# GLA layer of a two-block transformer: modulation of the first 128 features on TensorE, load order, and order of the projections

## Chip, cores and metric

The kernel runs on one core of one Trainium2 chip. The metric is the device time of one execution in microseconds (us); lower is better. A change of 0.2% is about what three runs can tell from none.

## The reference, cut to what matters

Five layers run one after the other over a sequence of 512 rows of 1024 features: gated linear attention (GLA), a gated MLP with a short convolution, a retention layer, a shared key/value projection with latent attention, and their norms. Only the first, GLA, is touched. What it computes, shortened:

```
cs = silu(c)                                          # 1024 numbers
shift, scale, gate = split(cs @ mod_w[0,0] + mod_b[0,0], 3)
h = x * (1 + scale) + shift                           # (512, 1024)
q, k, v, r, a_lr = split(h @ w_in, [512, 1024, 2048, 3072])
log_a = log_sigmoid(a_lr @ w_a2 + b_a) / 16           # the gates, 4 heads x 128
q_dec = q * 128**-0.5 * exp(cumsum(log_a)); k_inv = k * exp(-cumsum(log_a))
o = causal(q_dec k_inv^T) v + q_dec S                 # S: state carried from chunk to chunk, per head
u = o * rsqrt(mean(o*o) + 1e-5) * norm_g * silu(r)    # heads of 256 columns
y = layer_norm(2**0.25 * x + (1 + gate) * (u @ w_o))
```

All products keep FP32 accuracy: each operand is split into a high and a low part in the FP32R format, and three matmuls (high x high, high x low, low x high) make one product.

## The kernel before

Engines run side by side, each through its own instruction stream in a fixed order; a scheduler places the instructions when the kernel is built, by priority in program order and by its own estimates, so an instruction that the program writes later may run in a gap of an earlier part. The order in which the Python code issues the parts is therefore the lever that the change pulls.

**Matrix products.** `mm3` (L152) issues the three matmuls, at L154, L155 and L156. `wload` (L120) loads 512 KB of weights into a `raw` tile on the SP queue (L127), and `split` (L107) makes the high part by a cast on ScalarE (L114) and the low part by a subtraction on VectorE (L115) into a `wsp` tile. There are four `raw` and four `wsp` buffers (L266), and each is reused in program order: a load waits until the tile four places back has been consumed. `proj_t` (L169) multiplies four blocks of 128 rows by 512 weight columns into four accumulators `acc`; `proj_f` (L201) makes tiles of 128 features by 512 rows. After the first stage there are four `acc` and four `aux` PSUM banks. A projection of 512 columns is 96 matmuls of 512 columns.

**The first stage** is `gla_start` (L484): eight slices k of 128 features. For each, `loads` (L494) issues the slice of the modulation weights `ms` (two halves of 512 KB, L498), of the transposed input `xq` (256 KB, L499) and of `l_w` (512 KB, L501), which holds the weight columns of v (heads 0 and 1), and of q and k (heads 0 and 1). `operand` (L504) computes scale and shift of the 128 features on VectorE, as a sum over `ms` times the row `csr` = silu(c), broadcast to all partitions (L508), adds the bias `mb` into `mc` (L510, L511) and lets ScalarE make the high part of the operand, `hT`, and the full value `xv` (L516); L517 makes the low part. `weights` casts and splits `raw`. Then come 24 matmuls into eight accumulators. `setup` (L296) loads `csr` first of all and applies silu to it (L301); `setup_late` (L310) loads and transforms `cs`, the same numbers as columns, after the stage.

**The rest of GLA** is issued by `gla` (L382) in this order: `gla_a` (the 16 gate columns), `gla_decay` (L581: the gate chain, that is exp, ln, scan and exp on ScalarE and VectorE for four heads), `gla_r` of pair 0 with its Silu on ScalarE (L418), `vectors` (L317), `gla_prep` of heads 0 and 1, `gla_inner` of head 0 (L640), `gla_qk` of head 2, `gla_inner` of head 1, `gla_qk` of head 3, `gla_outer` of heads 0 and 1 (L672), `gla_prep` of 2 and 3, `gla_v` of pair 1, `gate_T` of pair 0 (transposes, L442, and splits, L117 and L118), `gla_inner` of 2 and 3, `gla_r` of pair 1 (L462), the reload of x (L466), `gla_outer` of 2 and 3, `gate_T` of pair 1, and the output projection in `post_mod` (L692). `gla_inner` has a serial part: the state `sf` goes from chunk to chunk (L665, L666) and is split into `st`.

Between these, `place` (L402) hands out ten pieces of modulation work: eight chunks for the next layer, each two loads of 512 KB into `raw` and two VectorE sums (L411), and two gate chunks of 512 columns (`mod_chunk`, L349), each four loads and eight VectorE steps (L362). `PLACE` (L269) says how many go where.

Of the kernel before, what the change touches and what calls it, by code (L numbers as in the profile page):

```python
# [18 lines left out]
P = 128  # L19
T = 512  # L20
# [47 lines left out]
def layouts(ins):  # L68
# [4 lines left out]
    def mod(i):  # L73
# [5 lines left out]
    m0, m1 = mod(0), mod(1)  # L79
    return {"l_ba": np.ascontiguousarray(ins["gla_b_a"][0].reshape(4, P).T),  # L80
            "l_x": np.ascontiguousarray(ins["x"][0].T),
            "l_mod": m0[0], "l_modb": m0[1], "l_mod1": m1[0], "l_modb1": m1[1],
# [14 lines left out]
class Kern:  # L97
# [168 lines left out]
    RAW, WSP, ST, MS = 4, 4, 6, 4  # L266
    GATES = {0: 4, 1: 5, 2: 6, 3: 7}
    WOUT = {6: (0, 2), 7: (2, 4)}
    PLACE = (0, 2, 0, 2, 2, 2, 2)  # L269
# [26 lines left out]
    def setup(self, ph):  # L296
        nc, a = self.nc, self.a
        cr = a["c"][0]
        self.csr = self.mod.tile([P, D], F32, name="csr")
        nc.sync.dma_start(self.csr, bass.AP(tensor=cr.tensor, offset=cr.offset, ap=[[0, P], [1, D]]))  # L300
        nc.scalar.activation(self.csr, self.csr, AF.Silu)  # L301
# [7 lines left out]

    def setup_late(self, ph):  # L310

        nc, a = self.nc, self.a
        self.cs = self.cons.tile([P, 8], F32, name="cs")
        nc.sync.dma_start(self.cs, a["l_c"])
        nc.scalar.activation(self.cs, self.cs, AF.Silu)
# [66 lines left out]
    def gla(self):  # L382
        nc, a, tc = self.nc, self.a, self.tc
        w = a["gla_w_in"][0]
        with ExitStack() as ctx:
# [38 lines left out]
            with tc.tile_pool(name="gla_core", bufs=1, reuse_waits="tile") as ph:  # L424
# [6 lines left out]
                def prep(h):  # L431
                    return self.gla_prep(ph, decay[h], raw[h])
# [13 lines left out]
                p0 = prep(0)  # L446
                p1 = prep(1)
                place(3)
                i0 = self.gla_inner(ph, p0, vh(0), tril)
                raw += self.gla_qk(xT, (2,))  # L450
                i1 = self.gla_inner(ph, p1, vh(1), tril)
                raw += self.gla_qk(xT, (3,))
# [9 lines left out]
                self.gla_r(xT, 1, lambda b, ps: nc.scalar.activation(u[1][:, b, :], ps, AF.Silu))  # L462
                place(6)
                for b in range(NB):
                    self.res[b] = self.main.tile([P, D], F32, tag=f"res{b}", name=f"res{b}")
                    nc.sync.dma_start(self.res[b], a["x"][0, b * P:(b + 1) * P, :])  # L466
                outer(2, i2)
# [13 lines left out]
            self.post_mod(lambda n: (uP, self.wsubs(a["gla_w_o"][0], n * 512, n * 512 + 512,  # L481
                                                    pool=self.tail if n else None)), 8, gate, True, A, B)

    def gla_start(self, ph, out):  # L484
# [4 lines left out]
        accs = [self.acc() for _ in range(8)]  # L489
        mb = ph.tile([P, 8, 2], F32, name="mb")  # L490
        nc.sync.dma_start(mb, a["l_modb"].rearrange("p (k j) -> p k j", j=2))
# [818 lines left out]
```

## Time and profile before

| what | us |
|---|---|
| median of 3 runs | 1260.5 |
| lowest and highest run | 1259.19 and 1261.57 |
| the profiled execution, its own time | 1261.78 |
| its span, from the first to the last instruction | 1260.0 |
| TensorE (PE) busy | 1225.5 (97% of the span) |
| VectorE (DVE) busy | 817.6 (65%) |
| ScalarE (ACT) busy | 535.3 (42%) |
| DMA | 118 GB/s mean over the span |

The profile is of one execution; 1.8 us of its time lie outside the span. PE counts matmuls, PEld the loading of their stationary operand, SPq the issue of DMAs on the SyncE queue. PEclk is the granted TensorE clock as a part of 2.4 GHz (0.5 is 1.2 GHz). In a timeline a line is: start, duration, engine, source line, operation, output<-inputs, count, and in brackets the idle time before it with what ended it. A line marked x4 merges four instructions that follow each other.

### The profile page before, as it was taken

To read this page: it belongs to the slowest core of one execution; us is meant where nothing else is said; L and a number is where in the kernel's file an instruction comes from. 1 tells how busy PE (TensorE), PEld (TensorE's weight loads), DVE (VectorE), ACT (ScalarE), POOL (GpSimd) and SP (SyncE) were. 2 spreads that over 40 slices of the span, in tenths; PEclk is the share of its full clock that TensorE was granted. 3 is DMA by queue.
4 is the path that set the end of the run, shared out by engine and by line. 5 is a ranking of instruction groups with operands and counts; after the bars stand their busy time and mean duration, and the time that the engine had idled before them with its cause. 6 is when DMAs were issued, how large, how long until landed. Compare 5 with 4: busy or idle time off the path is not lost.

```text
span 1260.0 us, 16047 instructions
## 1 busy us (share of the span) xinstructions
PE 1225.5 (97%) x5982; PEld 1024.9 (81%) x5982; DVE 817.6 (65%) x1836; ACT 535.3 (42%) x946; POOL 3.7 (0%) x15
## 2 busy tenths in 40 slices
PE   5989999999999999999999999999999999999997
PEld 4767877898888888888788888888888888888886
DVE  5698877788442354445875649556454689687755
ACT  3583444533332223341543333433434347577631
POOL 0000000000000000000000000000000000000000
PEclk9998999999999999999999999999999999999999
DMA  9658554147322333333152332323332333212221
GB/s 346 213 171 258 168 195 134 51 125 226 97 90 98 101 99 89 97 134 117 66 158 86 88 90 82 92 85 92 117 106 96 109 98 107 69 50 78 84 84 68
DMA packets 133043, 148.44 MB, mean 118 GB/s; under 512 B 9825, under 2 KB 92152, under 8 KB 132964
## 3 DMA queue, kind: packets, MB, share of 16 engines
q1 hardware_dynamic: 132964, 147.40, 36.5%
q8 instruction: 47, 0.77, 0.3%
q14 instruction: 32, 0.26, 0.1%
HBM read 141.09 MB, written 6.29 MB: 117 GB/s over the span
## 4 chain that ended last, share of the span: by engine, by line
PE 86%; DVE 7%; ACT 4%; DMA 2%; issue 2%; SPq 0%; DVEq 0%; ACTq 0%
PE acc L154 25%; PE acc L156 25%; PE acc L155 25%; PE po L154 1%; PE po L156 1%; PE po L155 1%; PE aux L154 1%; PE aux L156 1%; PE aux L155 1%; DMA raw<-in_gla_w_in 1%; DVE wsp L115 1%; PE aux L899 1%; DMA ms<-in_l_mod 1%; ACT wsp L114 1%; PE aux L1251 1%
## 5 line engine op out<-in xcount | busy, mean ns | idle before, releaser
L115 DVE TENSOR_TENSOR wsp<-raw,wsp 128x1024 fp32r<-128x1024 f32 (+1 forms) x162 | 195.5, 1208 | 192.4 <-ACT wsp L114 192.1
L114 ACT CAST wsp<-raw 128x1024 fp32r<-128x1024 f32 (+1 forms) x162 | 167.9, 1039 | 289.5 <-PE acc L156 253.6
L154 PE MATMUL acc<-hT,wsp 128*128 128x512 f32 (+1 forms) x640 | 244.8, 382 | 0.5 <-DVE v L115 0.5
L156 PE MATMUL acc<-hT,wsp 128*128 128x512 f32 (+1 forms) x640 | 243.7, 381 | 0.0
L155 PE MATMUL acc<-hT,wsp 128*128 128x512 f32 (+1 forms) x640 | 243.3, 380 | 0.0
L154 PE MATMUL acc<-wsp,hT 128*128 128x512 f32 (+2 forms) x448 | 170.0, 386 | 14.6 <-ACT wsp L114 14.6
L155 PE MATMUL acc<-wsp,hT 128*128 128x512 f32 (+2 forms) x448 | 171.6, 383 | 0.0
L156 PE MATMUL acc<-wsp,hT 128*128 128x512 f32 (+2 forms) x448 | 170.3, 382 | 0.0
L154 PEld LDWEIGHTS acc<-hT,wsp 128*128 128x128 f32 x640 | 121.2, 189 | 23.7 <-DVE v L115 1.4
L155 PEld LDWEIGHTS acc<-hT,wsp 128*128 128x128 f32 x640 | 120.9, 189 | 22.1 <-issue 0.2
L156 PEld LDWEIGHTS acc<-hT,wsp 128*128 128x128 f32 x640 | 120.8, 189 | 22.0
L154 PEld LDWEIGHTS acc<-wsp,hT 128*128 128x128 f32 x448 | 84.7, 189 | 29.9 <-ACT wsp L114 14.6
L156 PEld LDWEIGHTS acc<-wsp,hT 128*128 128x128 f32 x448 | 84.6, 189 | 15.1
L155 PEld LDWEIGHTS acc<-wsp,hT 128*128 128x128 f32 x448 | 84.7, 189 | 14.4 <-DVE wsp L115 0.3
L154 PE MATMUL acc<-wsp,uT 128*128 128x512 f32 (+1 forms) x192 | 75.3, 392 | 0.0
L156 PE MATMUL acc<-wsp,uT 128*128 128x512 f32 (+1 forms) x192 | 75.2, 392 | 0.0
L155 PE MATMUL acc<-wsp,uT 128*128 128x512 f32 (+1 forms) x192 | 74.9, 390 | 0.0
L154 PE MATMUL acc<-wsp,p 128*128 128x512 f32 x144 | 56.9, 395 | 0.0
L155 PE MATMUL acc<-wsp,p 128*128 128x512 f32 x144 | 56.9, 395 | 0.0
L156 PE MATMUL acc<-wsp,p 128*128 128x512 f32 x144 | 56.9, 395 | 0.0
L801 DVE SCALAR_TENSOR_TENSOR cv<-acc,cols,cv 128x511 f32<-128x511 f32 x22 | 16.5, 749 | 57.7 <-ACT cv L800 57.7
L800 ACT ACTIVATE cv<-acc,cols 128x512 f32<-128x512 f32 x22 | 17.2, 780 | 82.4 <-PE acc L156 82.4
(357 smaller groups left out, 2062.1 us busy)
## 6 DMA issues: line engine op xcount, KB each, us to landing
raw<-in_w_in_a SPq DMA_DIRECT2D x48, 512.0 KB
raw<-in_ffn_w_up SPq DMA_DIRECT2D x44, 512.0 KB
raw<-in_ffn_w_down SPq DMA_DIRECT2D x22, 512.0 KB
ms<-in_l_mod SPq DMA_DIRECT2D x16, 512.0 KB
raw<-in_gla_w_in SPq DMA_DIRECT2D x16, 512.0 KB
rawm<-in_l_mod SPq DMA_DIRECT2D x16, 512.0 KB
rawm<-in_mod_w SPq DMA_DIRECT2D x16, 512.0 KB
raw<-in_w_out_a SPq DMA_DIRECT2D x16, 512.0 KB
```

Source lines behind the costliest of these rows:

```text
L114: nc.scalar.copy(hi, src)
L115: nc.vector.tensor_sub(lo, src, self.f(hi))
L154: mm(out, l[0], r[0], start=first, stop=False)
L155: mm(out, l[0], r[1], start=False, stop=False)
L156: mm(out, l[1], r[0], start=False, stop=last)
L800: nc.scalar.activation(t, p, AF.Identity, scale=cw[2 * NT + j], bias=cb[j])
L801: nc.vector.scalar_tensor_tensor(t[:, 1:], p[:, :T - 1], cw[NT + j], t[:, 1:], op0=OP.mult, op1=OP.add)
L899: nc.tensor.transpose(pu[:, b * P:(b + 1) * P], u[:, b, i * P:(i + 1) * P], self.ident)
L1251: nc.tensor.matmul(sc[:, :n], qrT[i][:, s], kr[i][:, :n], start=False, stop=i == 1)
```

## The change

Six edits, all in GLA. (1) The scale and shift of the first 128 features are computed on TensorE: a new array `l_f0` holds the modulation weights of these features as eight blocks of 128 inputs for scale and eight for shift, and 16 plain F32 matmuls of one column multiply them with `cs`. `setup_late` goes; `cs` and the bias `mb` are loaded on ScalarE's queue at the start. (2) The SP queue of the start takes `l_f0` (two halves), the first slice of x, the first weight slice in two halves, and only then `csr`; the first slice's casts are done in halves and its matmuls ordered by the part that is ready. (3) Twelve matmuls of 512 columns on a constant tile run ahead of the first loads' arrival (`WARM`). (4) `gla_qk` of heads 2 and 3 moves in front of `gla_prep` of 0 and 1; `gla_r` of pair 1 moves from behind `gla_inner` of 3 to behind `gla_inner` of 1. (5) The first half of the output projection's first 512 columns (features from pair 0) is issued between `gla_inner` of 3 and `gla_outer` of 2, into accumulators that `post_mod` then goes on with. (6) `PLACE` changes from (0, 2, 0, 2, 2, 2, 2) to (2, 0, 0, 0, 3, 3, 2).

```diff
--- before.py
+++ after.py
@@ -77,8 +77,10 @@
         return np.ascontiguousarray(both), np.ascontiguousarray(bias.transpose(1, 0, 2).reshape(P, 16))
 
     m0, m1 = mod(0), mod(1)
+    f0 = np.concatenate([ins["mod_w"][0, 0][:, 1024:1024 + P], ins["mod_w"][0, 0][:, 0:P]], 1)
     return {"l_ba": np.ascontiguousarray(ins["gla_b_a"][0].reshape(4, P).T),
             "l_x": np.ascontiguousarray(ins["x"][0].T),
+            "l_f0": np.ascontiguousarray(f0.reshape(8, P, 2 * P).transpose(1, 0, 2).reshape(P, 16 * P)),
             "l_mod": m0[0], "l_modb": m0[1], "l_mod1": m1[0], "l_modb1": m1[1],
             "l_c": np.ascontiguousarray(ins["c"].reshape(8, P).T),
             "l_w": np.ascontiguousarray(np.concatenate([w[:, 1024:1536], w[:, 0:256], w[:, 512:768]], 1))}
@@ -264,9 +266,10 @@
 
 
     RAW, WSP, ST, MS = 4, 4, 6, 4
+    WARM = 12
     GATES = {0: 4, 1: 5, 2: 6, 3: 7}
     WOUT = {6: (0, 2), 7: (2, 4)}
-    PLACE = (0, 2, 0, 2, 2, 2, 2)
+    PLACE = (2, 0, 0, 0, 3, 3, 2)
 
     def run(self):
         tc, nc = self.tc, self.nc
@@ -295,10 +298,10 @@
 
     def setup(self, ph):
         nc, a = self.nc, self.a
-        cr = a["c"][0]
         self.csr = self.mod.tile([P, D], F32, name="csr")
-        nc.sync.dma_start(self.csr, bass.AP(tensor=cr.tensor, offset=cr.offset, ap=[[0, P], [1, D]]))
-        nc.scalar.activation(self.csr, self.csr, AF.Silu)
+        self.cs = self.cons.tile([P, 8], F32, name="cs")
+        nc.scalar.dma_start(self.cs, a["l_c"])
+        nc.scalar.activation(self.cs, self.cs, AF.Silu)
         self.ident = self.cons.tile([P, P], F32, name="ident")
         make_identity(nc, self.ident)
         self.rstd = self.cons.tile([P, NB], F32, name="rstd")
@@ -306,13 +309,6 @@
         nc.gpsimd.memset(self.ones, 1.0)
         self.res = [None] * NB
         self.col = {}
-
-    def setup_late(self, ph):
-
-        nc, a = self.nc, self.a
-        self.cs = self.cons.tile([P, 8], F32, name="cs")
-        nc.sync.dma_start(self.cs, a["l_c"])
-        nc.scalar.activation(self.cs, self.cs, AF.Silu)
 
     def vectors(self, ph):
 
@@ -443,13 +439,12 @@
                         self.split(t[:, 0, i, :], t[:, 1, i, :], pu, scale=self.c("norm_g")[i % 2])
                     return t
 
-                p0 = prep(0)
-                p1 = prep(1)
+                raw += self.gla_qk(xT, (2, 3))
                 place(3)
+                p0, p1 = prep(0), prep(1)
                 i0 = self.gla_inner(ph, p0, vh(0), tril)
-                raw += self.gla_qk(xT, (2,))
                 i1 = self.gla_inner(ph, p1, vh(1), tril)
-                raw += self.gla_qk(xT, (3,))
+                self.gla_r(xT, 1, lambda b, ps: nc.scalar.activation(u[1][:, b, :], ps, AF.Silu))
                 place(4)
                 outer(0, i0)
                 outer(1, i1)
@@ -459,11 +454,13 @@
                 uT = [gate_T(0)]
                 i2 = self.gla_inner(ph, p2, vh(2), tril)
                 i3 = self.gla_inner(ph, p3, vh(3), tril)
-                self.gla_r(xT, 1, lambda b, ps: nc.scalar.activation(u[1][:, b, :], ps, AF.Silu))
                 place(6)
                 for b in range(NB):
                     self.res[b] = self.main.tile([P, D], F32, tag=f"res{b}", name=f"res{b}")
                     nc.sync.dma_start(self.res[b], a["x"][0, b * P:(b + 1) * P, :])
+
+                accs = [self.acc() for _ in range(NB)]
+                self.proj_t(self.pair_of(uT), self.wsubs(a["gla_w_o"][0], 0, 512, 0, 4), 512, None, accs=accs)
                 outer(2, i2)
                 outer(3, i3)
                 uT.append(gate_T(1))
@@ -478,8 +475,9 @@
             nc.vector.tensor_mul(B, self.col["ln_b0"], mc1[:, :, 0])
             nc.vector.tensor_add(B, B, mc1[:, :, 1])
             gate = self.mod_gate([mods[0, 2048], mods[0, 2560]])
-            self.post_mod(lambda n: (uP, self.wsubs(a["gla_w_o"][0], n * 512, n * 512 + 512,
-                                                    pool=self.tail if n else None)), 8, gate, True, A, B)
+            wo = a["gla_w_o"][0]
+            first = ((k + 4, w) for k, w in self.wsubs(wo, 0, 512, 4, 8))
+            self.post_mod(lambda n: (uP, self.wsubs(wo, 512, 1024, pool=self.tail) if n else first), 8, gate, True, A, B, accs=accs)
 
     def gla_start(self, ph, out):
 
@@ -487,13 +485,54 @@
         nc, a = self.nc, self.a
         tl, xT = self.new_hT()
         accs = [self.acc() for _ in range(8)]
+
+        warm = ph.tile([P, T], F32R, tag="t2", name="warm", bufs=2)
+        nc.vector.tensor_copy(warm, self.ones[:, 0:1].to_broadcast([P, T]))
+        for _ in range(self.WARM):
+            nc.tensor.matmul(accs[7], warm[:, :P], warm, start=True, stop=True)
         mb = ph.tile([P, 8, 2], F32, name="mb")
-        nc.sync.dma_start(mb, a["l_modb"].rearrange("p (k j) -> p k j", j=2))
         xs = [self.main.tile([P, 2, T], F32, tag=f"res{q}", name=f"xq{q}") for q in range(4)]
+
+        def first():
+
+            m = ph.tile([P, 8, 2, P], F32, tag="ms", name="m0", bufs=self.MS)
+            f0 = a["l_f0"].rearrange("p (k j f) -> p k j f", k=8, j=2)
+            raw = self.main.tile([P, self.WN], F32, tag="raw", name="raw", bufs=self.RAW)
+            for k in (0, 4):
+                nc.sync.dma_start(m[:, k:k + 4], f0[:, k:k + 4])
+            nc.scalar.dma_start(mb, a["l_modb"].rearrange("p (k j) -> p k j", j=2))
+            nc.sync.dma_start(xs[0][:, 0], a["l_x"][0:P])
+            halves = [slice(0, 512), slice(512, D)]
+            for h in halves:
+                nc.sync.dma_start(raw[:, h], a["l_w"][0:P, h])
+            cr = a["c"][0]
+            nc.sync.dma_start(self.csr, bass.AP(tensor=cr.tensor, offset=cr.offset, ap=[[0, P], [1, D]]))
+            pm = [accs[6 - j][:, 0:1] for j in range(2)]
+            for k in range(8):
+                for j in range(2):
+                    nc.tensor.matmul(pm[j], m[:, k, j], self.cs[:, k:k + 1], start=k == 0, stop=k == 7)
+            mc = self.small(2, "mc")
+            nc.vector.tensor_scalar(mc[:, 0:1], pm[0], mb[:, 0, 0:1], 1.0, op0=OP.add, op1=OP.add)
+            nc.vector.tensor_add(mc[:, 1:2], pm[1], mb[:, 0, 1:2])
+            hi, lo = tl[0][:, 0, 0, :], tl[0][:, 1, 0, :]
+            sp = self.main.tile([P, 2, self.WN], F32R, tag="wsp", name="wsp", bufs=self.WSP)
+            v = ph.tile([P, T], F32, tag="t2", name="xv", bufs=2)
+            nc.scalar.activation(hi, xs[0][:, 0], AF.Identity, scale=mc[:, 0:1], bias=mc[:, 1:2])
+            for h in halves:
+                nc.scalar.copy(sp[:, 0, h], raw[:, h])
+                nc.vector.tensor_sub(sp[:, 1, h], raw[:, h], self.f(sp[:, 0, h]))
+            nc.scalar.activation(v, xs[0][:, 0], AF.Identity, scale=mc[:, 0:1], bias=mc[:, 1:2])
+            nc.vector.tensor_sub(lo, v, self.f(hi))
+            parts = [([t[:, b * P:(b + 1) * P] for t in xT.k[0]], [sp[:, i, 0:512] for i in range(2)]) for b in range(NB)]
+            parts += [([sp[:, i, 512 + j * P:640 + j * P] for i in range(2)], xT.k[0]) for j in range(4)]
+            order = [[(0, 0), (0, 1), (1, 0)]] * NB + [[(0, 0), (1, 0), (0, 1)]] * 4
+            for t in range(3):
+                for acc, (l, r), o in zip(accs, parts, order):
+                    nc.tensor.matmul(acc, l[o[t][0]], r[o[t][1]], start=t == 0, stop=False)
 
         def loads(k):
             r = slice(k * P, k * P + P)
-            m = ph.tile([P, 2, D], F32, tag="ms", name="ms", bufs=4)
+            m = ph.tile([P, 2, D], F32, tag="ms", name="ms", bufs=self.MS)
             for j in range(2):
                 nc.sync.dma_start(m[:, j], a["l_mod"][r, j * D:(j + 1) * D])
             nc.sync.dma_start(xs[k // 2][:, k % 2], a["l_x"][r])
@@ -521,15 +560,17 @@
             self.split(sp[:, 0], sp[:, 1], raw)
             return sp
 
-        for k in range(8):
+        first()
+        nc.scalar.activation(self.csr, self.csr, AF.Silu)
+        for k in range(1, 8):
             m, raw = loads(k)
             operand(k, m)
             sp = weights(raw)
             wv = [sp[:, i, 0:512] for i in range(2)]
             for b in range(NB):
-                self.mm3(accs[b], [t[:, b * P:(b + 1) * P] for t in xT.k[k]], wv, k == 0, k == 7)
+                self.mm3(accs[b], [t[:, b * P:(b + 1) * P] for t in xT.k[k]], wv, False, k == 7)
             for j in range(4):
-                self.mm3(accs[4 + j], [sp[:, i, 512 + j * P:640 + j * P] for i in range(2)], xT.k[k], k == 0, k == 7)
+                self.mm3(accs[4 + j], [sp[:, i, 512 + j * P:640 + j * P] for i in range(2)], xT.k[k], False, k == 7)
         v = out.tile([P, 2, NB, 512], F32R, tag="v", name="v")
         for b in range(NB):
             self.split(v[:, 0, b, :], v[:, 1, b, :], accs[b])
@@ -539,7 +580,6 @@
             for j in range(2):
                 nc.scalar.copy(raw[:, j], accs[4 + 2 * j + h])
             raws.append(raw)
-        self.setup_late(ph)
         return xT, v, raws
 
     def gla_v(self, out, xT, pr):
@@ -689,7 +729,7 @@
         for b in range(NB):
             nc.vector.scalar_tensor_tensor(u[:, b], out[b], rs[:, b:b + 1], u[:, b], op0=OP.mult, op1=OP.mult)
 
-    def post_mod(self, src, nk, gate, alpha, A, B=None, affine=None):
+    def post_mod(self, src, nk, gate, alpha, A, B=None, affine=None, accs=None):
 
 
 
@@ -741,7 +781,7 @@
                 self.res_rstd(b)
 
         xP, subs = src(0)
-        self.proj_t(xP, subs, 512, lambda b, p: z_half(b, 0, p), nk=nk)
+        self.proj_t(xP, subs, 512, lambda b, p: z_half(b, 0, p), nk=nk, accs=accs)
         xP, subs = src(1)
         self.proj_t(xP, subs, 512, lambda b, p: (z_half(b, 1, p), finish(b)), nk=nk, tail=4)
 
```

## Rows read from the trace of the kernel before

**Rows 1.** The page, busy time (us), share of the span and instructions of TensorE.

```profile
PE 1225.5 (97%) x5982; PEld 1024.9 (81%) x5982; DVE 817.6 (65%) x1836; ACT 535.3 (42%) x946; POOL 3.7 (0%) x15
```

**Rows 2.** Waits of TensorE, whole span: waiter, releaser, total us, times, longest.

```profile
PE acc L154 <- ACT wsp L114: 14.6, 1, 14.6
PE aux L154 <- ACT ki L114: 4.2, 1, 4.2
PE aux L154 <- ACT kt L114: 2.6, 1, 2.6
...
PE aux L154 <- DVE sf L665: 0.7, 1, 0.7
```

**Rows 3.** Stretches of 2 us: busy us of PE, PEld, DVE, ACT, POOL, PEclk, DMA.

```profile
90.00:92.00 2.00, 0.01 (x1) 0.01 (x1) 2.00 (x5) 2.00 (x5) 0.00 (x0) 0.71 0.55 137
...
96.00:98.00 2.00, 2.00 (x11) 1.90 (x11) 1.33 (x4) 1.29 (x2) 0.00 (x0) 0.59 1.07 363
...
114.00:116.00 2.00, 1.65 (x8) 1.56 (x9) 2.00 (x4) 1.33 (x3) 0.00 (x0) 0.68 0.82 269
116.00:118.00 2.00, 2.00 (x8) 1.71 (x8) 1.33 (x3) 0.41 (x1) 0.00 (x0) 0.50 0.75 252
```

**Rows 4.** Timelines 0 to 26 us by engine: start, duration, engine, line, operation.

```profile
5.42 1.06 ACT L301 ACTIVATE csr<-csr 128x1024 f32<-128x1024 f32 x1 [3.41 <-DMA csr<-in_c]
...
9.21 1.23 DVE L508 SCALAR_TENSOR_TENSOR ms<-ms,csr 128x1024 f32<-128x1024 f32 x1 [9.21 <-DMA ms<-in_l_mod]
...
12.06 0.81 ACT L516 ACTIVATE hT<-xq,mc 128x512 fp32r<-128x512 f32 x1 [5.59 <-DVE mc L511]
...
13.48 1.03 ACT L114 CAST wsp<-raw 128x1024 fp32r<-128x1024 f32 x1
...
14.56 2.08 PE L154 MATMUL acc<-wsp,hT 128*128 128x512 f32 x4 [14.56 <-ACT wsp L114]
...
17.96 0.81 ACT L516 ACTIVATE hT<-xq,mc 128x512 fp32r<-128x512 f32 x1 [3.45 <-DVE mc L511]
...
19.38 1.04 ACT L114 CAST wsp<-raw 128x1024 fp32r<-128x1024 f32 x1
...
22.27 1.07 PE L154 MATMUL acc<-wsp,hT 128*128 128x512 f32 x4
...
25.29 1.99 ACT L114 CAST wsp<-raw 128x1024 fp32r<-128x1024 f32 x2
```

**Rows 5.** Timeline of TensorE round 632 us, two plain F32 products of 128 columns.

```profile
632.46 0.61 PE L776 MATMUL aux<-diag,ones 128*128 128x128 f32 x4
```

**Rows 6.** Timeline of TensorE and ScalarE where the gate chain ends.

```profile
87.46 0.38 PE L342 MATMUL aux<-ident,rows 128*128 128x128 f32 x2
91.99 0.48 PE L154 MATMUL aux<-qd,ki 128*128 128x128 f32 x1 [4.15 <-ACT ki L114]
...
87.56 1.28 ACT L418 ACT_TABLE_LOAD   x1
88.86 2.06 ACT L418 ACTIVATE u<-acc 128x512 f32<-128x512 f32 x4
```

**Rows 7.** Timeline of ScalarE ahead of the wait at 111.8 us.

```profile
111.58 1.04 ACT L114 CAST wsp<-raw 128x1024 fp32r<-128x1024 f32 x1 [1.50 <-DMA raw<-in_gla_w_in]
...
113.82 0.47 ACT L114 CAST kt<-aux 128x384 fp32r<-128x384 f32 x1
```

**Rows 8.** Timeline of heads 2 and 3: TensorE, the DMA queue and VectorE.

```profile
156.50 0.33 PE L154 MATMUL aux<-qd,ki 128*128 128x128 f32 x1
...
185.87 0.29 PE L154 MATMUL po<-v,at 128*128 128x256 f32 x1
...
167.27 22.35 SPq L127 DMA_DIRECT2D raw<-in_gla_w_o  x8
...
177.76 0.42 DVE L115 TENSOR_TENSOR st<-sf,st 128x256 fp32r<-128x256 f32 x1
...
201.49 1.40 DVE L118 SCALAR_TENSOR_TENSOR uT<-aux,cols,uT 128x512 fp32r<-128x512 f32 x2
```

## The prediction

> **What bounds the kernel now.** I read the page's busy times first. TensorE is busy for 1225.5 of the 1260.0 us span [rows 1], so the change can only gain where TensorE stands still or runs at the lower clock; VectorE (65%) and ScalarE (42%) matter where they are what TensorE waits for. The table of waits says where it stands still [rows 2]: 14.6 us before its first matmul, then 4.2 us for the high part of k (`ki`) and 2.6 us for a cast of `kt`; the rest are waits of 0.7 us and less. The windows of 2 us add the clock [rows 3]. At 90 to 92 us PEclk is 0.71, so 1.16 us of that stretch were at half clock; it stays there until about 97.6 (0.59 in the last stretch is 1.64 us at half). TensorE came back to work at 91.99 [rows 6], so it worked 5.6 us at half clock, which costs 2.8 us beside the 4.15 of the gap. After the gap of 2.55 us the clock is at half from 114.7 to at least 118.0: 3.3 us, 1.6 us lost. At the start the timeline shows the same without a clock row: four matmuls take 2.08 us at 14.56 and 1.07 us at 22.27 [rows 4], and the 24 matmuls of the first slice fill 7.7 us where 24 x 0.227 = 5.4 would do (0.227 is 1.07 less one duration of about 0.39, over three). All of this lies in the layer that the change edits, and it makes up nearly everything there is to win.
>
> **The start (edits 1 to 3).** Before, the first half of `ms` is there at 9.21, two sums of 1.23 and the bias steps follow, the operand's high part starts at 12.06, its full value and the whole 1.03 us cast come next, and the first matmul is at 14.56 [rows 4]. After, the two halves of `l_f0` are as many bytes as `csr` and the first half of `ms` were, and head the queue with no bias load between; I take 9.0 for the landing of the second. Eight one-column products remain then. Two plain F32 products show as four instructions in 0.61 us, 0.11 apart [rows 5], so these are 16 instructions, 1.8 us. That row has 128 columns, not one; I bound the price by 0 (all hidden behind the landing) and 3.5 us (twice the pitch, at half clock). The scale and shift take 0.4 as before (9.21 + 2 x 1.23 to 12.06), the high part 0.8, and half a cast 0.5: first matmul at about 12.7, and at full clock the first slice ends at 18.1.
>
> Then the second slice is late. Its sums need `csr`, whose silu of 1.06 us [rows 4] now stands on ScalarE behind the first slice's high part, two half casts and full value: 11.3 + 0.8 + 1.0 + 0.8 = 13.9, silu to 15.0, two sums to 17.5, high part at 17.9. Before it started at 17.96 and the cast behind it ended 2.5 us later, at 20.4 [rows 4]; so the second slice is ready at 20.3, where before TensorE reached it at 22.27. That is 2.0 us gained, and TensorE waits from 18.1 to 20.3. If the warm-up's clock is lost again, the first slice takes 7.7 us and ends at 20.4: nothing is lost by it. The third slice's cast ended 5.9 us after the second's (26.3 against 20.4), more than the 5.4 that TensorE needs: 0.5 us of waiting that the late start used to hide. **Start: 1.5 us gained**, between a loss of 0.2 (the one-column products at their upper price) and a gain of 6.0 (they are hidden and the second slice does not wait for `csr`); I stay near the low end since the path through `csr` is followed row by row. The twelve matmuls, their constant and the two loads on ScalarE's queue lie in time in which TensorE and ScalarE did nothing; without that cover the twelve would cost 12 x 0.43 = 5 us.
>
> **The gate chain (edits 4 and 6).** The 4.15 us gap ends when `ki` is there, after the gate chain on ScalarE and VectorE [rows 6]. The 96 matmuls of `gla_qk` for heads 2 and 3 (96 x 0.227 = 21.8 us, as for any projection of 512 columns) now stand in front. But they need `acc` banks, and all four hold the sums of `gla_r`, which ScalarE empties with a Silu that stands behind the chain's last exps and a table load of 1.28 us: the first of four is done at 88.86 + 0.6 = 89.5, while TensorE's last other work starts at 87.46 [rows 6]. So a wait of 2.0 us takes the place of the 4.15; behind it in TensorE's queue stand all of `gla_qk` and the inner products. ScalarE must also cast four weight tiles for `gla_qk`, 1.04 each [rows 4], in that time; how many fall into the chain's own gaps the trace can't show. Bounds are none and four (4.2 us); I take one, so 3.0 us of waiting. A gap of that size is nearest to the 2.55 one, so I add its 1.6 us of half clock. **Gate chain: 6.95 before, 4.6 after, 2.3 gained**, between 4.95 gained (2.0 us, no lower clock) and 2.1 lost (6.2 + 2.8).
>
> The table load is 1.28 us in the trace and the Silu starts 0.02 us behind it [rows 6]. The Trainium skill ("ScalarE: Activation LUTs", section "What ACT_TABLE_LOAD costs") gives 2.66 us for a switch, with a drain of 1.38; by it the bank would come free 1.4 us later and the term would shrink to 0.9. This trace has no such drain, and the row decides.
>
> **Heads 0 and 1 (edits 4 and 6).** The 2.55 us gap comes from a `kt` cast that stands on ScalarE behind a weight cast that itself waited 1.50 us for its load [rows 7]; in program order that load stands behind the four of `place(3)`. `PLACE` now puts none there, and `gla_r` of pair 1, 21.8 us of matmuls, may fill the gaps. **3.8 of the 4.15 us gained** (2.55 and 1.6), bounds 0 and 4.15.
>
> **Heads 2 and 3 (edits 4 to 6).** This is the bill. From their first inner product at 156.50 to the last split of `uT` at 202.9 [rows 8] lie 46.4 us, with one wait of 0.7 [rows 2]. 21.8 of them are `gla_r`, which leaves; 23.9 us of other TensorE work stay, among them the half output projection (48 matmuls, 10.9 us), which edit 5 lets fill earlier gaps, and 5.4 us that can follow the first half of `uT`: 29.3. How long is the chain without `gla_r`? The states were ready at 178.2, yet `gla_outer` began at 185.87 [rows 8], because `gla_r` had TensorE: 38.7 at most. I take off 3 for the splits of `gla_r`'s weights that VectorE no longer makes amid it (about as long as ScalarE's 1.04 each) and 3 to 4 for the outer products, which no longer share TensorE with the output projection (an estimate from 10.9 us spread over them): 32. So 2.7 us of waiting for 0.7: **2.0 lost**, bounds 0.7 gained (29.3 or shorter) and 8.7 lost (38.7). I take the value nearer the short end because the gaps are small and many, so no lower clock is added.
>
> **Sum.** 1.5 + 2.3 + 3.8 - 2.0 = 5.6 us off the profiled execution's 1261.78, so 1256.2. The median of the runs is 1.3 below that execution: 1254.9, said as 1255.0.
>
> **Rivals.** *All covers hold:* the second slice does not wait for `csr` (4.5), the gate chain waits 2.0 at full clock (4.95), heads 0 and 1 give 4.15 and heads 2 and 3 gain 0.7: 14.3, so 1246.2. For it speaks that each cover is long enough (21.8 us against gaps of 2 to 4), against it that both new waits have an exact cause above. *The waits only move:* start and gate chain give nothing, as where four casts land in the chain or the one-column products are slow: 3.8 - 2.0 = 1.8, so 1258.7. *Slower:* the half output projection's weights come too late to fill. They need `raw` buffers behind all eight loads of the two gate chunks, and were issued only at 167.27, 10.8 us after the first inner product [rows 8]; `place(5)` now hands out one chunk more, 2 sums of 1.23 us, so 13.2, and some 3.5 until cast and split. TensorE then has about 6 us of inner products in nearly 17 us: 10.5 of waiting and 2.8 of half clock, 12.6 lost after the 0.7 of before. With the other three terms that is 5.0 us slower: 1265.5. It decides once the loss there passes 7.6. Against it: `gla_r`'s weights no longer hold the buffers during `gla_v`, so the chunks can be eaten earlier.
>
> **Chances.** Forecast 0.42 (its own range 1251 to 1259), all covers 0.20, waits only move 0.20, slower 0.18. The range 1246 to 1264 leaves out half of the slower case and the low end of the best one. 0.2% is 2.5 us, about what a measurement can tell from none: faster means below 1258.0, slower above 1263.0. Faster: 0.40 + 0.20 + 0.07 = 0.67; slower 0.16; same 0.17.
>
> **What would show it.** Right: the first weight matmul near 12.7 and a wait of about 2 us ahead of the second slice with a sum or `csr` behind it; a wait of 2 to 4 us of `gla_qk`'s first matmul for `u`; no wait for `kt` of heads 0 and 1; waits of a few us in all between the inner products of heads 2 and 3. Wrong: no wait at `gla_qk`, or a TensorE wait on the output projection's weights, or a first matmul later than 14.

## The result: 10 us slower, and the profile after

The changed kernel takes 1270.8 us (median of 4 runs, 1269.59 to 1271.58) against 1260.3 (median of 4 as well): a ratio of 1.0081, interval 1.0069 to 1.0094. The forecast was 1255.0 with a range of 1246 to 1264. The profiled execution took 1269.59 us with a span of 1267.8, so 7.8 more than that of before. Nearly all of it arises in GLA: the next layer's first matmul is at 249.77 us, where it was at 242.25, so 7.5 later, and behind it the two traces are alike.

The page's busy times of the changed kernel:

```profile
PE 1237.4 (98%) x6026; PEld 1033.4 (82%) x6026; DVE 814.4 (64%) x1834; ACT 535.7 (42%) x947; POOL 4.0 (0%) x15
```

PE is busy for 12 us more than in [rows 1], though almost none of its work is new: a matmul at half clock counts as busy for longer, and the twelve constant matmuls fill time that was idle. "98%" is no sign of health.

TensorE's waits over the whole span (waiter, releaser, total us, times, longest):

```profile
PE aux L156 <- DVE af L697: 3.0, 2, 2.9
PE acc L531 <- ACT wsp L522: 2.3, 1, 2.3
PE acc L156 <- ACT uT L119: 2.3, 2, 1.9
PE aux L641 <- DVE a L618: 2.0, 1, 2.0
PE acc L157 <- DVE wsp L117: 1.8, 1, 1.8
PE po L156 <- ACT scr L725: 1.7, 2, 1.0
...
```

The two large gaps of [rows 2], for `ki` and `kt`, are gone, and the 14.6 us of the start are filled (its first weight matmul comes 1.5 us earlier). In their place stand several middling ones. The 2 us stretches show which of them cost clock as well (columns as in [rows 3]):

```profile
68.00:70.00 2.00, 2.00 (x6) 1.52 (x6) 2.00 (x4) 2.00 (x4) 0.00 (x0) 0.50 0.81 297
...
124.00:126.00 2.00, 2.00 (x10) 1.93 (x10) 1.90 (x5) 1.12 (x3) 0.00 (x0) 0.50 0.98 350
...
184.00:186.00 2.00, 2.00 (x9) 1.81 (x10) 2.00 (x3) 0.48 (x1) 0.00 (x0) 0.50 0.00 0
```

Summed over neighbouring stretches, the clock is at half for 3.4 us round 69, 6.8 round 125 and 3.4 round 185; half of each is lost. At the start it is at half for another 6.8 us, from 9.5 to 16.3.

**Start.** Timeline of TensorE, the changed kernel:

```profile
6.59 4.17 PE L513 MATMUL acc<-cs,m 128*128 128x1 f32 x32
13.08 2.07 PE L531 MATMUL acc<-wsp,hT 128*128 128x512 f32 x4 [2.31 <-ACT wsp L522]
...
20.14 1.07 PE L156 MATMUL acc<-wsp,hT 128*128 128x512 f32 x4
...
59.15 0.39 PE L158 MATMUL acc<-hT,wsp 128*128 128x512 f32 x1
60.78 3.90 PE L614 MATMUL acc<-hT,was 128*32 128x512 f32 x16 [1.24 <-ACT qk L581]
```

The second slice begins at 20.14 for 22.27 [rows 4], but the stage ends only 1.0 us earlier (59.54 for 60.51), and `gla_a` then waits 1.24 us until ScalarE has emptied the accumulators of q and k, a wait that the kernel before did not have (there it began at 60.35). Even the 1.0 us is not shown to be the edits' doing. The last matmul of the stage, in the kernel before and in the run qk_only below, whose start is that of before:

```profile
60.12 0.39 PE L156 MATMUL acc<-hT,wsp 128*128 128x512 f32 x1
```

```profile
58.55 0.39 PE L156 MATMUL acc<-hT,wsp 128*128 128x512 f32 x1
```

With the same start the stage ends 1.6 us earlier in the second execution, so a single trace can't tell a gain of 1.0.

**Gate stage.** The DMA queue, first of the kernel before, then of the changed one, and then the changed kernel's TensorE:

```profile
45.87 5.67 SPq L127 DMA_DIRECT2D raw<-in_gla_w_in  x4
```

```profile
60.23 5.81 SPq L129 DMA_DIRECT2D raw<-in_gla_w_in  x4
```

```profile
66.64 1.35 PE L641 MATMUL aux<-a,wr 96*128 96x512 f32 x4 [1.97 <-DVE a L618]
...
88.67 0.50 PE L157 MATMUL acc<-wsp,hT 128*128 128x512 f32 x1 [1.79 <-DVE wsp L117]
```

These are the four weight loads of `gla_r`, pair 0. `PLACE` now hands out two chunks ahead of it, whose four loads fill the `raw` ring, so the weights are asked for 14 us later. `gla_r` is no longer there to run between `gla_a` and the gate chain, its casts fall into the chain, and it ends at 93.5 instead of 87.6.

**Heads 0 and 1.** VectorE, then TensorE:

```profile
115.76 1.23 DVE L407 SCALAR_TENSOR_TENSOR rawm<-rawm,csr 128x1024 f32<-128x1024 f32 x1 [0.84 <-DMA rawm<-in_l_mod]
...
118.38 1.23 DVE L407 SCALAR_TENSOR_TENSOR rawm<-rawm,csr 128x1024 f32<-128x1024 f32 x1 [0.77 <-DMA rawm<-in_l_mod]
...
119.53 1.22 DVE L117 TENSOR_TENSOR wsp<-raw,wsp 128x1024 fp32r<-128x1024 f32 x1
120.66 0.68 DVE L697 TENSOR_TENSOR af<-aux,tril 128x512 f32<-128x512 f32 x1
```

```profile
116.67 0.48 PE L156 MATMUL acc<-wsp,hT 128*128 128x512 f32 x1
...
121.40 0.39 PE L156 MATMUL aux<-v,kt 128*128 128x256 f32 x1 [2.87 <-DVE af L697]
```

The sums of `place(4)` (L407) stand on VectorE ahead of `af`, two of them waiting for their own loads. And of the 96 matmuls of `gla_r` of pair 1, meant as cover, four run before the matmul that waits; the rest stand behind it in TensorE's order.

**Heads 2 and 3.** ScalarE and TensorE of the changed kernel:

```profile
176.74 1.05 ACT L116 CAST wsp<-raw 128x1024 fp32r<-128x1024 f32 x1 [1.63 <-PE acc L158]
177.69 2.04 ACT L116 CAST v<-acc 128x512 fp32r<-128x512 f32 x4
179.60 2.46 ACT L119 ACTIVATE uT<-aux,cols 128x512 fp32r<-128x512 f32 x4
...
180.37 0.50 PE L156 MATMUL acc<-wsp,uT 128*128 128x512 f32 x1 [1.93 <-ACT uT L119]
...
182.63 0.33 PE L156 MATMUL aux<-qd,ki 128*128 128x128 f32 x1 [1.53 <-DVE uT L120]
```

A weight cast for the output projection waits for its `wsp` buffer, which `gla_v`'s last matmuls hold, and the casts of `v` and `uT` queue behind it. In the kernel before, the four casts of `v` followed the four blocks one by one, from 150.21 on, and the splits of `uT` were in time.

### The profile page after: what moved, and what is told of

It is laid out like the page before. It is cut to its first block, busy times and chain, and to the rows that moved or that the text cites. A ratio compares the mean times of both kernels' runs of the same rounds, so it can differ in the third digit from the quotient of the medians.

```text
span 1267.8 us, 16152 instructions
## 1 busy us (share of the span) xinstructions
PE 1237.4 (98%) x6026; PEld 1033.4 (82%) x6026; DVE 814.4 (64%) x1834; ACT 535.7 (42%) x947; POOL 4.0 (0%) x15
## 4 chain that ended last, share of the span: by engine, by line
PE 74%; DVE 4%; ACT 2%; issue 1%; DVEq 0%; ACTq 0%
PE acc L158 22%; PE acc L156 22%; PE acc L157 22%; PE po L156 1%; PE po L158 1%; PE po L157 1%; PE aux L156 1%; PE aux L158 1%; PE aux L157 1%; PE aux L939 1%; PE aux L1291 1%; PE aux L1313 1%; ACT p L1298 0%; DVE wsp L117 0%; DVE rs_t L238 0%
## 5 line engine op out<-in xcount | busy, mean ns | idle before, releaser
L156 PE MATMUL acc<-hT,wsp 128*128 128x512 f32 (+1 forms) x636 | 241.9, 380 | 0.6 <-DVE v L117 0.6
L157 PE MATMUL acc<-hT,wsp 128*128 128x512 f32 (+1 forms) x636 | 241.1, 379 | 0.0
L158 PE MATMUL acc<-hT,wsp 128*128 128x512 f32 (+1 forms) x636 | 240.7, 379 | 0.0
L157 PE MATMUL acc<-wsp,hT 128*128 128x512 f32 (+2 forms) x444 | 169.7, 382 | 1.8 <-DVE wsp L117 1.8
L156 PE MATMUL acc<-wsp,hT 128*128 128x512 f32 (+2 forms) x444 | 168.0, 387 | 0.5 <-ACT wsp L116 0.4
L158 PE MATMUL acc<-wsp,hT 128*128 128x512 f32 (+2 forms) x444 | 168.2, 382 | 0.0
L156 PEld LDWEIGHTS acc<-hT,wsp 128*128 128x128 f32 x636 | 119.7, 188 | 23.3 <-DVE v L117 1.4
L158 PEld LDWEIGHTS acc<-hT,wsp 128*128 128x128 f32 x636 | 119.7, 188 | 22.1
L157 PEld LDWEIGHTS acc<-hT,wsp 128*128 128x128 f32 x636 | 119.7, 188 | 22.1 <-issue 0.2
L157 PEld LDWEIGHTS acc<-wsp,hT 128*128 128x128 f32 x444 | 83.8, 189 | 16.3 <-DVE wsp L117 2.2
```

What stands on the lines that cost most here:

```text
L156: mm(out, l[0], r[0], start=first, stop=False)
L157: mm(out, l[0], r[1], start=False, stop=False)
L158: mm(out, l[1], r[0], start=False, stop=last)
```

## The experiments

Times are medians; before is 1259.8 to 1260.4 us, measured anew beside each group of runs, and a difference is the ratio less one, times 1260, with the ends of its interval.

**start_only** and **order_only** cut the change in two: edits 1 to 3 on the kernel before, and edits 4 to 6 on it. Each is shown against the changed kernel:

```diff
-    PLACE = (2, 0, 0, 0, 3, 3, 2)
+    PLACE = (0, 2, 0, 2, 2, 2, 2)
...
```

and the order and output projection of before (start_only); the start of before (order_only):

```diff
-        first()
-        nc.scalar.activation(self.csr, self.csr, AF.Silu)
-        for k in range(1, 8):
+        for k in range(8):
```

> The kernel before with edits 1 to 3 alone (the start), its own order, PLACE and output projection. Theory: the start is worth what the trace of the changed kernel shows at the end of the first stage, 1.0 us (59.54 for 60.51), and the wait of gla_a for the evictions (1.24 us) can give all of it back: 1258.8 to 1260.5, so 0.0 to 1.5 us faster than before. Rival: the start is what made the change slower, through the clock that falls to half from 9.7 to 16.5 us or through later work that it shifts: 1263 or more.

> The kernel before with edits 4 to 6 alone (order, half output projection, PLACE), with its own start. Theory: all of the loss is here, and a little more than the whole change shows since the start's gain is missing: 1270 to 1273. Rival: start and order only hurt together (the start shifts the casts that the gate chain meets): 1261 to 1266.

start_only: 1260.8, +1.0 us (-0.1 to +2.0). order_only: 1267.7, +7.8 (+6.3 to +9.3). Most of the loss is in the order; the start gains nothing. Both miss what was expected: start_only is just above its 1258.8 to 1260.5, and order_only is below its 1270 to 1273, so the order alone costs some 2.4 us less than the whole change, at the edge of the two intervals, and whether the start costs more together with the new order stays open. TensorE of start_only:

```profile
91.89 0.47 PE L156 MATMUL aux<-qd,ki 128*128 128x128 f32 x1 [3.93 <-ACT ki L116]
...
114.66 0.39 PE L156 MATMUL aux<-v,kt 128*128 128x256 f32 x1 [1.97 <-ACT kt L116]
```

The wait of 1.24 us ahead of `gla_a` is there too (at 60.87), and order_only and qk_only, with the old start, don't have it: it comes from the start edits. The two old gaps are back.

**place0_back** moves the first two chunks behind `gla_r` again.

```diff
-    PLACE = (2, 0, 0, 0, 3, 3, 2)
+    PLACE = (0, 2, 0, 0, 3, 3, 2)
```

> The changed kernel with PLACE (0, 2, 0, 0, 3, 3, 2) for (2, 0, 0, 0, 3, 3, 2): the first two chunks stand behind gla_r of pair 0 again, so that its four weight loads are no longer queued behind four chunk loads. Theory: gla_r's weights are there before gla_a, its matmuls run ahead of pz as before, and the waits of 1.97 (pz) and 1.79 (wsp) and 1.7 us of half clock go; in their place gla_qk's first matmul waits 2 to 3 us for acc banks behind the Silu. Net 2.5 to 5 us faster than the changed kernel: 1266 to 1268.5. Rival: the loss comes from heads 0 to 3 alone, or the chunks only move in front of gla_qk's loads: 1270 to 1272.

1267.6: +6.9 (+5.2 to +8.7), 3 us less than the changed kernel. Its TensorE shows the wait that the prediction had meant:

```profile
90.03 0.50 PE L156 MATMUL acc<-hT,wsp 128*128 128x512 f32 x1 [1.87 <-ACT u L414]
...
178.33 0.50 PE L156 MATMUL acc<-wsp,uT 128*128 128x512 f32 x1 [0.81 <-ACT uT L119]
```

The waits of 1.97 and 1.79 are gone; `gla_qk` waits 1.87 for a bank, with 3.4 us at half clock. That is 3.6 lost for 5.5. Another 1.1 us is at heads 2 and 3 (0.81 for 1.93), while the wait for `af` is 0.6 longer.

**r1_back** moves `gla_r` of pair 1 back.

```diff
-                self.gla_r(xT, 1, ...)
                 place(4)
...
+                self.gla_r(xT, 1, ...)
                 place(6)
```

> The changed kernel with gla_r of pair 1 behind gla_inner of head 3 again, where it stood before. Theory: its 21.8 us of matmuls again cover the splits of uT and the second gate_T, so 6 of the 7 us that the changed kernel lost between 176 and 250 us come back; heads 0 and 1 lose a filler and wait up to 2 us more: 1265 to 1268. Rival: those stalls have another cause (the half output projection uses up the filler either way, or casts bunch on ScalarE): 1270 to 1273.

1267.0: +6.8 (+5.2 to +8.4), so some 3.5 us less. The waits for `uT` of 1.93 and 1.53 are gone and the next two are 0.41 and 0.77, much as before (0.48 and 0.66); in heads 0 and 1 the wait for `af` stays 2.86, with or without its filler.

**chunks_late** takes the sums out of heads 0 and 1.

```diff
-    PLACE = (2, 0, 0, 0, 3, 3, 2)
+    PLACE = (2, 0, 0, 0, 0, 6, 2)
```

> The changed kernel with PLACE (2, 0, 0, 0, 0, 6, 2) for (2, 0, 0, 0, 3, 3, 2): the three chunks handed out after heads 0 and 1 move behind gla_v, so that VectorE has no sum to execute ahead of af of head 0. Theory: the wait of 2.87 us for af and about 3.6 us lost to the half clock behind it (122 to 129.5 us) go, heads 0 and 1 gain 4 to 6.5 us; later sums can delay heads 2 and 3 by 0 to 2: 1265 to 1268. Rival: af is late because of the casts and splits of gla_r's weights on VectorE, or because its bank's input is late: the wait stays, 1270 to 1273.

1268.0: +7.6 (+6.0 to +9.1). TensorE:

```profile
123.98 0.39 PE L156 MATMUL aux<-v,kt 128*128 128x256 f32 x1 [0.95 <-ACT kt L116]
...
178.08 0.48 PE L156 MATMUL aux<-qd,ki 128*128 128x128 f32 x1 [3.34 <-DVE uT L120]
```

The wait for `af` and the half clock round 125 are gone, so the sums made them. Part of that is paid back at 178 (3.34, and the clock at half from about 177 to 184, so 3.4 lost; in the changed kernel 1.93, 1.53 and 1.7): the steps of the gate chunks, whose loads now queue behind those of six chunks, run until 189 us instead of 175, and one stands on VectorE ahead of the splits of `v` and `uT`:

```profile
176.02 0.74 DVE L358 SCALAR_TENSOR_TENSOR macc<-rawm,cs,macc 128x512 f32<-128x512 f32 x1
...
177.28 2.71 DVE L120 SCALAR_TENSOR_TENSOR uT<-aux,cols,uT 128x512 fp32r<-128x512 f32 x4
```

**no_half** undoes edit 5.

```diff
-                accs = [self.acc() for _ in range(NB)]
-                self.proj_t(self.pair_of(uT), self.wsubs(a["gla_w_o"][0], 0, 512, 0, 4), 512, None, accs=accs)
```

> The changed kernel without edit 5: the whole output projection behind gate_T of pair 1 as before, everything else as changed. Theory: the half projection is what TensorE has left to fill heads 2 and 3 with, so without it the idle time there grows by 4 to 8 us: 1275 to 1279. Rival: the half projection starts only when uT is there and holds the queue (the two waits of 1.93 and 1.53 for uT and the two po waits of 1.74 in all are its doing), so without it the time is the same or lower: 1266 to 1271.

1268.8: +8.3 (+6.8 to +9.8), 2 us less, with intervals that overlap: the rival, the same or lower. TensorE:

```profile
181.25 0.50 PE L156 MATMUL acc<-wsp,uT 128*128 128x512 f32 x1 [1.93 <-ACT uT L119]
```

The first half of the output projection starts at the same place without edit 5, because the scheduler moves it there by itself. The edit only fixes it ahead of `gla_outer`; the two `po` waits of 1.7 us in all come with it and go with it. The waits for `uT` stay. In this trace the clock is at half for 6.8 us round 187 (3.4 in the changed kernel) and `af` is waited for 3.65 us (2.87), which takes back what the two waits give; that the edit costs 2 us is not shown.

**qk_only** puts `gla_qk` of heads 2 and 3 in front of `gla_prep` in the kernel before, nothing else.

```diff
-                p0 = prep(0)
-                p1 = prep(1)
+                raw += self.gla_qk(xT, (2, 3))
                 place(3)
+                p0, p1 = prep(0), prep(1)
                 i0 = self.gla_inner(ph, p0, vh(0), tril)
-                raw += self.gla_qk(xT, (2,))
                 i1 = self.gla_inner(ph, p1, vh(1), tril)
-                raw += self.gla_qk(xT, (3,))
```

> The kernel before with one piece of edit 4 alone: gla_qk of heads 2 and 3 in front of gla_prep of 0 and 1, PLACE and everything else as before. By the prediction's terms the gate chain gains 2.3 us (a wait of about 2 us for acc banks with some half clock in place of 4.15 with 2.8), and heads 0 and 1 lose their filler. Theory: the gate chain's gain is real (3 to 4 us, as in the run with place(0) moved back: 1.87 us of waiting and 3.4 us at half clock), but the sums of place(3) and the weight splits stand ahead of af and a gap of 3 us with half clock opens in heads 0 and 1, so nothing is left: 1259 to 1263. Rival: heads 0 and 1 stay covered and the gain shows: 1256 to 1258.

1260.05: -0.1 (-1.3 to +0.9). At the gate chain it waits 2.11 us for a bank instead of 4.15 for `ki`, and in heads 0 and 1:

```profile
118.66 0.38 PE L154 MATMUL aux<-v,kt 128*128 128x256 f32 x1 [3.35 <-DVE af L655]
```

The clock is at half from about 119 to 126. What the gate chain gains, heads 0 and 1 lose.

**undo_three** undoes PLACE, the place of `gla_r` of pair 1, and edit 5 together (the diffs of r1_back and no_half, and PLACE as before).

```diff
-    PLACE = (2, 0, 0, 0, 3, 3, 2)
+    PLACE = (0, 2, 0, 2, 2, 2, 2)
```

> The changed kernel with three pieces undone together: PLACE of before, gla_r of pair 1 back behind gla_inner of 3, no half output projection. What is left of the change is the start and gla_qk in front of gla_prep. Theory: these three are the loss; taken singly they gave 3.2, 3.8 and 2.0 us, and with them gone the time is that of the two harmless pieces, each of which measured as no change by itself: 1259 to 1262. Rival: the pieces depend on one another, so that single gains do not add (gla_qk in front together with the changed start still loses): 1263 to 1267.

1262.6: +2.9 (+1.8 to +4.2), between the two. VectorE, then TensorE:

```profile
115.27 1.23 DVE L407 SCALAR_TENSOR_TENSOR rawm<-rawm,csr 128x1024 f32<-128x1024 f32 x1 [0.69 <-DMA rawm<-in_l_mod]
...
121.00 0.69 DVE L693 TENSOR_TENSOR af<-aux,tril 128x512 f32<-128x512 f32 x1
```

```profile
121.74 0.58 PE L156 MATMUL aux<-v,kt 128*128 128x256 f32 x1 [5.36 <-DVE af L693]
```

Nearly three quarters of the loss is gone. What is left is at one place: `af`, whose products were there at 114.4, behind sums that wait for their loads. The clock is at half for 10.2 us behind it. Two pieces that cost little or nothing alone, the start and `gla_qk` in front, cost 2.9 us together.

**warm0** leaves out the twelve constant matmuls.

```diff
-    WARM = 12
+    WARM = 0
```

> The changed kernel with WARM = 0, so without edit 3, the twelve matmuls on a constant. Theory: in the changed kernel the clock is at half from 9.7 to 16.5 us whatever they do, and the second slice is not ready before 19.9, so they are worth at most the 0.7 us by which a first slice of 7.7 us from 13.1 would end later: 1270.5 to 1272. Rival: they hold the clock or bring it back sooner and are worth 2 us or more: 1273 to 1275.

1271.1: +11.8 (+10.1 to +13.6), not to be told from the changed kernel's +10.2. TensorE:

```profile
5.40 6.99 PE L513 MATMUL acc<-cs,m 128*128 128x1 f32 x32 [5.40 <-ACT cs L304]
14.70 2.07 PE L531 MATMUL acc<-wsp,hT 128*128 128x512 f32 x4 [2.31 <-ACT wsp L522]
...
22.90 1.07 PE L156 MATMUL acc<-wsp,hT 128*128 128x512 f32 x4
```

Without them the one-column products take 6.99 us for 4.17, so the first weight matmul comes 1.6 us later, and the first slice takes 8.2 us for 7.1. The second slice begins 2.8 us later in all, and `gla_a` still 1.2 (61.96 for 60.78). So in the traces the twelve are worth more than the 0.7 us expected, but none of it is to be seen in the time.

**r1_mid** issues `gla_r` of pair 1 inside `gla_inner` of head 0, ahead of the products that wait.

```diff
...
+        if mid:
+            mid()
         st, sf = [], ph.tile([P, 256], F32, tag="sf", name="sf")
```

> The changed kernel with gla_r of pair 1 issued inside gla_inner of head 0, between the products that feed kt and af and those that use them, so that all 96 matmuls stand ahead of the matmul that waits. Theory (the cover stood behind the waiting matmul: only 4 of the 96 ran before it): the wait of 2.87 us and the 3.6 us lost to the clock behind it go, with 1 to 3 us given back in head 1, whose chain now has less behind it: 1265 to 1268. Rival (VectorE's sums are so late that no cover helps, or the wait moves whole to head 1): 1270 to 1273.

1267.7: +7.3 (+5.8 to +8.9). The wait for `af` of head 0 is gone: with the 96 in front, it is covered. Head 1, now without filler, pays:

```profile
146.19 0.90 PE L692 MATMUL aux<-ident,qk 128*128 128x128 f32 x3 [4.99 <-DVE sf L708]
```

The clock is at half for another 6.8 us round 148. So the cover was long enough and stood on the wrong side of the wait. Now one head takes it all.

**split_qk**, **split_qk2** and **fill_first** build a better version. split_qk has the changed start, `gla_qk` of head 2 in front of `gla_prep` and of head 3 between the inner products, `gla_r` of pair 1 and the output projection as before, PLACE (0, 2, 0, 0, 0, 6, 2). split_qk2 adds PLACE (0, 2, 0, 2, 0, 4, 2) and two of the four q and k evictions on VectorE. fill_first adds the hook of r1_mid, with half of head 3's `gla_qk` (`qk3`, its definition is left out here) in each head:

```diff
-                i0 = self.gla_inner(ph, p0, vh(0), tril)
-                raw += self.gla_qk(xT, (3,))
-                i1 = self.gla_inner(ph, p1, vh(1), tril)
...
+                i0 = self.gla_inner(ph, p0, vh(0), tril, lambda: qk3(0))
+                i1 = self.gla_inner(ph, p1, vh(1), tril, lambda: qk3(1))
```

> A version built from what the runs showed: the changed start; gla_qk of head 2 in front of gla_prep of 0 and 1, gla_qk of head 3 between the two inner products as a filler; gla_r of pair 1 back behind gla_inner of 3; no half output projection; PLACE (0, 2, 0, 0, 0, 6, 2), so no chunk stands in front of gla_r of pair 0 or between heads 0 and 1. Theory: the gate chain loses 3.6 us instead of 7, heads 0 and 1 and heads 2 and 3 at most what they lose before: 1254 to 1258, faster than both kernels. Rival: the six chunks behind gla_v bunch up in front of heads 2 and 3, or the 10.9 us of one head's gla_qk are used up before kt is there: 1260 to 1265.

> split_qk with two edits: PLACE (0, 2, 0, 2, 0, 4, 2), so that two of the six late chunks are summed in the gate chain and none is ahead of af of head 0, and the second halves of the q and k evictions at the end of the first stage on VectorE, so that gla_a need not wait 1.24 us for four copies on ScalarE. Theory: up to 1 us at gla_a and 1 to 2 us of the waits in heads 0 and 1 (1.17, 0.76 and 1.70) go: 1256 to 1258.5. Rival: the waits come from VectorE's total work in heads 0 and 1 and only move: 1259 to 1261.

> split_qk2 with one edit: the q tile and the k tile of gla_qk of head 3 (24 matmuls, 5.4 us each) stand inside gla_inner of heads 0 and 1, ahead of the matmuls that wait for kt and af. Theory: the waits of 2.32 and 1.02 us and the half clock from 106 to 110 us (1.7 us) go, and the states, which start up to 4 us later, delay gla_outer by at most 2: 1255 to 1258. Rival: the states' serial chain is what heads 0 and 1 wait for in the end, so that the waits move to gla_outer: 1259 to 1262.

split_qk 1259.3: -0.9 (-1.9 to +0.3); split_qk2 1259.0: -0.8 (-1.9 to +0.3), both misses, not to be told from before. fill_first **1257.7: -2.3 (-3.4 to -1.1)**, faster than both kernels. In split_qk2 TensorE still waited 2.32 us for `kt` at 105.4 with 44 of 48 filler matmuls behind the waiting one. TensorE's waits in fill_first:

```profile
PE acc L156 <- ACT u L414: 1.9, 1, 1.9
...
PE po L156 <- ACT scr L729: 1.6, 1, 1.6
...
PE po L156 <- DVE sf L709: 0.9, 1, 0.9
...
```

No wait for `kt` or `af` of heads 0 and 1 is left; part of it moved to `gla_outer` (1.6 and 0.9), as the rival said.

## Why the prediction was wrong

The forecast summed four terms to 5.6 us gained; the two profiled executions differ by 7.8 lost. The medians differ by 10.5: the profiled execution of before is 1.5 above its median and that of the changed kernel 1.2 below, and these 2.7 us are in no term here. Term by term, with half of each stretch at half clock counted as lost:

- **Start (1.5 gained; measured about 0.2 lost).** The first matmul came at 13.08 for 12.7 and the second slice at 20.14 for 20.3, there with no wait for its sums: the first slice ran in part at half clock and ended only then, as the text had allowed for. The stage ended 1.0 earlier, which other executions blur. The step that failed is that a gain there reaches the end: `gla_a` waits 1.24 us for evictions that the text did not look at. start_only, +1.0 (-0.1 to +2.0), bears it out.
- **Gate chain (2.3 gained; about 1.9 gained).** `gla_a`'s wait aside, the changed kernel loses 1.97 + 1.79 + 1.7 of clock = 5.5, the one before 0.4 (a wait ahead of the same products) + 4.15 + 2.8 = 7.4. The size came out, but by luck, not by the steps given: there was no wait at `gla_qk` at all, which the text had named as a sign of error. The step that failed: the text counted the loads of `place(3)` and of the gate chunks ahead of weights, but gave the two chunks that `place(0)` now hands out ahead of `gla_r` no cost. They put its weight loads off from 45.87 to 60.23 and its end from 87.6 to 93.5, past the Silu that `gla_qk` was to wait for. With that undone the predicted wait is there, 1.87 us, a cast less than the 3.0 of the text, and the clock costs 1.7 for 1.6. In the changed kernel the table load at 90.07 is 1.28 us once more, with the Silu 0.01 us behind it, so the 2.66 us that the Trainium skill gives for a switch ("ScalarE: Activation LUTs", "What ACT_TABLE_LOAD costs") are again not what the trace shows.
- **Heads 0 and 1 (3.8 gained; about 2.1 lost).** This is the largest miss. The step that failed: the text had `gla_r` fill the gaps wherever they lay, and `PLACE` put no loads there. But 2.87 us of waiting and 3.4 of clock took the place of 2.55 and 1.7. The scheduler brought the sums of `place(4)` forward, ahead of `af` (chunks_late shows that they made the wait), and 92 of the 96 matmuls stood behind the waiting one (r1_mid shows that they could have covered it).
- **Heads 2 and 3 (2.0 lost; about 6.5 lost).** The mechanism (waiting where `gla_r` had been the cover) was right, and the size of the term was off. The text took a chain of 32 us between bounds of 29.3 and 38.7, 2.7 us of waiting, and no lower clock, "because the gaps are small and many". The gaps were 1.93, 1.53, 0.54, 0.75 and 0.99, and the first two cost 1.7 of clock. r1_back shows that `gla_r`'s absence is the cause; no_half that edit 5, counted as a filler that the change provides, was one that the scheduler already had; it brings the two `po` waits (0.75 and 0.99).

These four terms make 6.9 of the 7.8; the other 0.9 is not traced. The rival *slower* gave 1265.5 through late weights of the output projection. Its sign was right, its mechanism not: the first of these weights was loaded in time (its cast ended at 172.3), and what came late was `uT`.

The single undoings (place0_back, r1_back, chunks_late, no_half) give about 3, 3.5, 2.5 and 2 us of a loss of 10, and undo_three 7; since intervals are 1.5 us to either side, how far they overlap stays open.

## What to carry to other kernels

A filler covers a wait only if it stands ahead of the waiting instruction in that engine's order: look at which matmuls run just before the wait, not at how much work is nearby, and put the filler between the producer and the consumer in program order. Side work handed out "somewhere later" takes buffers and queue places now, so a moved load or sum has to be followed through the ring it shares and through the in-order engine that executes it. Look first at what the scheduler already does: the half output projection that edit 5 issues by hand stood there without it, and no run shows a gain from it.

## What was not expected of the hardware

How much clock a gap costs can't be read from its length. With the 4.15 us for `ki` came 6.8 us at half clock in the kernel before (1.2 of them within the gap); in start_only, with 3.93 us at the same place, 10.2 (PEclk 0.50 in every stretch from 90 to 100), while its 1.97 us for `kt` cost none:

```profile
98.00:100.00 2.00, 2.00 (x8) 1.71 (x8) 1.80 (x3) 1.47 (x3) 0.00 (x0) 0.50 0.73 207
114.00:116.00 2.00, 1.34 (x9) 1.25 (x10) 2.00 (x5) 1.65 (x4) 0.00 (x0) 1.00 0.96 278
```

And the one-column products at the start did not hold the clock that the twelve matmuls had left: it fell from 1.00 to half at about 9.5 us, in a stretch in which TensorE counts as busy throughout (2.00 of 2.00 us):

```profile
8.00:10.00 2.00, 2.00 (x18) 2.00 (x18) 0.00 (x0) 0.00 (x0) 0.00 (x0) 0.87 1.02 415
```

Lastly, a wait and the clock ahead of it can be two shares of one delay. r1_back has the instructions of the changed kernel in the same order up to 88 us, and the same gap of 1.97 us, but behind it no lower clock:

```profile
66.72 1.20 PE L641 MATMUL aux<-a,wr 96*128 96x512 f32 x4 [1.97 <-DVE a L618]
...
88.76 0.50 PE L157 MATMUL acc<-wsp,hT 128*128 128x512 f32 x1 [3.38 <-DVE wsp L117]
```

```profile
68.00:70.00 2.00, 2.00 (x10) 1.68 (x9) 2.00 (x4) 2.00 (x4) 0.00 (x0) 1.00 0.77 274
```

The wait for the last weights of `gla_r` is 3.38 us here and 1.79 in the changed kernel, yet it ends at 88.76 and 88.67: TensorE came 1.6 us earlier to weights that were ready at the same time. So the 1.7 us of clock round 69 put off nothing behind 88.7 us in the changed kernel; without it the wait would have been that much longer. A wait has to be read together with the clock before it, and with when its releaser is done.
